# The first stage of a two-layer hybrid backbone: the modulation sums of each quarter are turned between two tiles

## The chip, the core and the metric

The kernel runs on one core of a Trainium2 chip. The core has a matrix engine (TensorE, PE in the profile; its weight loads are PEld), a vector engine (VectorE, DVE), a scalar engine (ScalarE, ACT), GpSimd (POOL) and a sync engine (SyncE, SP) that here only issues loads. Each engine takes its instructions in a fixed order of its own, and they wait for each other by semaphores. The metric is the device time of one execution in microseconds; smaller is better.

## What is computed

Two layers over 512 latent and 256 context tokens of width 1024. The part that matters here is the beginning of layer 0:

```python
sc, scc = silu(c), silu(c_ctx)
m_lat = split(sc @ mod_w[0] + mod_b[0], 6)          # shift, scale, gate, shift, scale, gate
m_ctx = split(scc @ mod_w[0] + mod_b[0], 6)
h_ctx = rms(x_ctx, norm_pre_mix[0]) * (1 + m_ctx[1]) + m_ctx[0]
h_lat = rms(x_lat, norm_pre_mix[0]) * (1 + m_lat[1]) + m_lat[0]
...
gq, gk, gv, gog, gz, aq, ak, av = split(concat(h_ctx, h_lat) @ even_w_in[0], EVEN_SIZES)
```

Behind it come gated linear attention and grouped-query attention side by side, an output projection, a SwiGLU feed-forward, and a second layer with a recurrent mixer (HGRN2) and its feed-forward. All of that stays as it is.

## The kernel before

Tokens lie in six tiles of 128: 0 to 3 are latent, 4 and 5 context. The channels of the 1024 inputs lie in eight blocks `k` of 128, and two blocks make a *quarter* `qd`. To keep float32 accuracy with a faster matmul type, each operand is held as a rounded part H and a remainder L, and a product is three matmuls (`mm3`, line 776): H with H, H with L, L with H. H of a token operand (`x` in the profile) is cast by ACT (`put`, L734) and L subtracted by DVE (L735). H and L of a weight (`wH`, `wL`) are made by ACT (L769) and DVE (L770) from a loaded `raw` buffer.

The first stage (`run`, L1904 to L1989) overlaps three things by quarters:

- `loads(qd)`: SP issues the loads of the modulation weights (`mraw`) and one unit of input weights, for all four quarters at once.
- `sums(qd, ks)`: TensorE sums shift and scale of both streams for this quarter's two channel blocks over the eight input blocks `ks`, 4 matmuls for each (the float32 ones are two passes, so the profile counts 8), into `mod_acc`. Behind the last, `mod_cols` (L465) has DVE copy the sums to `modrows` (L469) and returns a function that makes the *turn*: a transpose on TensorE (`modT`, shown with line 358) and DVE's adding of the bias into `modcol` (L481).
- `apply(qd)`: makes the turn by calling that function (L1942), then DVE forms the factor `aff` (L1945), DVE and ACT scale and shift the quarter's channels of the normalized tokens `xT` (L1954, L1952), and `put` splits the result into H and L.
- `z(t0, qd)`: the products of two token tiles `t0`, `t0`+1 with the quarter's two channel blocks, 2 tiles x 2 blocks x 3 = 12 matmuls of 128 x 288, summed over the quarters in `nat`. The 288 columns are the gates' low-rank input and half of the attention queries.

The last quarter's products are called from `even_mixer` (L1101): behind each pair of tiles ACT copies the results out (`zn` L1103, `natq` L1104). Then come constants for later (`late_constants`, L410): ACT issues the loads of `rows` and of `masks_f`, TensorE transposes the rows (`pt_rows`), DVE copies them to `col` (L408) and casts `masks` (L426); `lower_bounds` (L428) computes with `lb_tmp`. Then the mixer runs pieces in an order that is written out (L1219): `qk0` is two weight units of 1024 columns and the products `gqk`; `m` is one step of sums on DVE (`mod_vec`, L515) for the later modulation vectors: each load `mraw` of 128 x 1024 is multiplied by a column of `scT` and added to two sums `macc` (L535 the first, L537 the others). After eight blocks TensorE adds the sums over the partitions, DVE copies them (`modrows` again, 128 x 512), and TensorE transposes them (`modT` x4).

What sets the order: with `self.pinned` on, TensorE's instructions keep the order of the program (`pin`, L348). The other engines' instructions are placed by the compiler's scheduler, which estimates when each can run; on an engine the order is then fixed. Buffers are few: `raw` has 3, `wH` and `wL` 4 each, the modulation loads of the mixer 3, and a load is issued when its buffer's last reader is done.

## Time and profile before

| what | value |
|---|---|
| three runs | 1681.48, 1681.66, 1682.79 us; median 1681.66 |
| the profiled execution | 1680.08 us, of which the span from the first to the last instruction is 1678.3 us |
| TensorE's mean granted clock | 0.999 |
| transposes and statistics of the input, until the first sums | 0 to 20.6 us |
| the changed stage | 20.6 to 54.8 us |
| the mixer's first products up to the first long turn | 54.8 to 104.8 us |

Rows of the timeline read: start in us, duration in us, engine, line, operation, written tile <- read tiles, partitions x elements and type, count, and in brackets the idle time of the engine ahead of it and what ended it. ACTq and SPq rows are issues of loads. Rows of equal instructions are merged: start of the first, time from there to the end of the last.

### The profile page before, as it was taken

The numbers are of one execution on the slowest core, as the hardware profiler recorded it, in microseconds if no ns is written. First come the engines' busy times: TensorE is split into PE (matmuls) and PEld (weight loads), VectorE is DVE, ScalarE is ACT, GpSimd is POOL, SyncE is SP. The second block draws the span as 40 slices with busy tenths as digits, with TensorE's granted clock in tenths as the row PEclk, the third lists the DMA queues.
The fourth block names the chain that finished last, engine by engine and source line by source line (L and its number), as shares of the span: only waits on it lengthen the run. The fifth ranks groups of instructions, "written<-read, shape, count | busy, mean of one in ns | idle before, by whom it ended". The sixth has DMA issues, their size and how long they took to land.

```text
span 1678.3 us, 32400 instructions
## 1 busy us (share of the span) xinstructions
PE 1638.8 (98%) x13347; PEld 1474.3 (88%) x13347; DVE 1312.2 (78%) x2104; ACT 916.9 (55%) x1560; POOL 122.6 (7%) x129
## 2 busy tenths in 40 slices
PE   6999998999999999999999999999999999999998
PEld 5889987888999999998887788888888899999886
DVE  4889768966898989778668648788775499987887
ACT  4745557846544443445447536566564565555564
POOL 1004210001000000002101000000000100000310
PEclk9999999999999999999999999999999999999999
DMA  9651002154253446249516542111115334433973
GB/s 331 193 155 41 2 28 101 52 198 152 90 151 101 134 148 193 78 136 222 101 56 210 193 132 64 52 54 50 52 56 159 117 113 122 115 101 101 223 166 138
DMA packets 184736, 204.77 MB, mean 122 GB/s; under 512 B 7143, under 2 KB 141837, under 8 KB 184589
## 3 DMA queue, kind: packets, MB, share of 16 engines
q1 hardware_dynamic: 173632, 181.82, 34.6%
q0 software_dynamic: 9024, 17.30, 5.9%
q10 hardware_dynamic: 1932, 3.59, 0.6%
q8 instruction: 104, 1.70, 0.4%
q14 instruction: 44, 0.35, 0.1%
HBM read 193.23 MB, written 9.46 MB: 121 GB/s over the span
## 4 chain that ended last, share of the span: by engine, by line
PE 84%; DVE 7%; ACT 4%; DMA 2%; issue 2%; POOL 1%; DVEq 0%; ACTq 0%; POOLq 0%
PE nat L355 12%; PE a L355 11%; PE ff L355 8%; PE E L355 8%; PE x L355 6%; PE oproj L355 6%; PE o L355 4%; PE b L355 4%; PE D L355 4%; PE pearly L355 3%; PE fq L355 3%; PE gqk L355 2%; PE q L355 2%; PE S L355 2%; PE poh L355 1%
## 5 line engine op out<-in xcount | busy, mean ns | idle before, releaser
L355 PE MATMUL nat<-wH,x 128*128 128x256 f32 (+2 forms) x968 | 226.1, 322 | 3.1 <-ACT x L734 2.6
L355 PEld LDWEIGHTS nat<-wH,x 128*128 128x128 f32 x968 | 162.0, 190 | 20.5 <-ACT x L734 4.2
L824 ACT CAST wH<-raw 128x1024 fp32r<-128x1024 f32 x120 | 124.9, 1051 | 99.0 <-DVE raw L849 37.6
L825 DVE TENSOR_TENSOR wL<-raw,wH 128x1024 fp32r<-128x1024 f32 x120 | 145.7, 1221 | 23.2 <-ACT wH L824 22.6
L355 PE MATMUL nat<-wL,x 128*128 128x256 f32 (+2 forms) x484 | 153.5, 317 | 1.8 <-DVE wL L770 1.8
L770 DVE TENSOR_TENSOR wL<-raw,wH 128x1024 fp32r<-128x1024 f32 (+1 forms) x83 | 98.7, 1198 | 49.7 <-ACT wH L769 49.0
L355 PE MATMUL ff<-x,wH 128*128 128x512 f32 (+1 forms) x512 | 127.7, 340 | 0.0
L769 ACT CAST wH<-raw 128x1024 fp32r<-128x1024 f32 (+1 forms) x83 | 84.9, 1035 | 70.6 <-PE ff L355 19.9
L668 POOL TENSOR_TENSOR rs<-ms,neghalf 128x1 f32<-128x1 f32 (+2 forms) x62 | 64.7, 1049 | 791.1 <-DVE ms L666 791.0
L355 PE MATMUL oproj<-wH,x 128*128 128x512 f32 x320 | 102.3, 396 | 0.6 <-ACT x L1290 0.6
L355 PEld LDWEIGHTS nat<-wL,x 128*128 128x128 f32 x484 | 92.1, 190 | 7.9 <-DVE wL L770 2.7
L355 PEld LDWEIGHTS ff<-x,wH 128*128 128x128 f32 x512 | 87.2, 190 | 10.0
L597 DVE SCALAR_TENSOR_TENSOR macc<-mraw,scT,macc 128x1024 f32<-128x1024 f32 x70 | 88.0, 1280 | 8.8 <-DMA mraw<-in_mod_w_dram 8.4
L355 PE MATMUL x<-wH,two 128*128 128x512 f32 x280 | 90.6, 392 | 0.8 <-DVE y L1801 0.7
L976 ACT COPY qkh<-arr 128x512 f32<-128x512 f32 x112 | 70.1, 642 | 36.4 <-DVE arr L981 32.2
L1723 POOL DMA_DIRECT2D t<-in_ffn_w_down_dram x36 | 41.8, 1198 | 637.2 <-DVE t L1762 337.5
L355 PE MATMUL ff<-x,wL 128*128 128x256 f32 (+1 forms) x256 | 86.2, 337 | 0.0
L849 DVE TENSOR_TENSOR raw<-raw 128x512 f32<-128x512 f32 x120 | 82.8, 690 | 2.8
L981 DVE TENSOR_TENSOR arr<-arr,f 128x512 f32<-128x512 f32 x112 | 74.2, 687 | 1.9 <-ACT qkh L976 0.3
L355 PEld LDWEIGHTS oproj<-wH,x 128*128 128x128 f32 x320 | 59.5, 188 | 12.8 <-ACT x L1290 1.1
L355 PE MATMUL E<-x,wH 128*128 128x384 f32 (+1 forms) x320 | 70.7, 310 | 0.0
L355 PE MATMUL b<-x,wH 128*128 128x384 f32 (+1 forms) x320 | 70.6, 310 | 0.0
(420 smaller groups left out, 4530.2 us busy)
## 6 DMA issues: line engine op xcount, KB each, us to landing
mraw<-in_mod_w_dram SPq DMA_DIRECT2D x80, 512.0 KB, 4.1
raw<-in_ffn_w_gate_dram SPq DMA_DIRECT2D x44, 512.0 KB, 4.8
raw<-in_ffn_w_up_dram SPq DMA_DIRECT2D x44, 512.0 KB, 4.4
raw<-in_odd_w_in_dram SPq DMA_DIRECT2D x40, 512.0 KB, 3.7
t<-in_ffn_w_down_dram POOLq DMA_DIRECT2D x30, 512.0 KB, 8.7
raw<-in_ffn_w_down_dram SPq DMA_DIRECT2D x28, 512.0 KB, 7.9
mraw<-in_mod_w_dram SPq DMA_DIRECT2D x32, 256.0 KB, 6.3
raw<-in_even_w_in_dram SPq DMA_DIRECT2D x16, 512.0 KB, 6.8
```

Source lines behind the costliest of these rows:

```text
L355: return self.pin(self.nc.tensor.matmul(*a, **k))
L597: nc.vector.scalar_tensor_tensor(a, u, w, a, op0=ALU.mult, op1=ALU.add)
L668: nc.gpsimd.tensor_tensor(rs, ms, self.neghalf.to_broadcast([P, w]), op=ALU.pow)
L769: nc.scalar.copy(H[:, :m], raw[:, :m])
L770: nc.vector.tensor_tensor(L[:, :m], raw[:, :m], H[:, :m].bitcast(F32), op=ALU.subtract)
L824: self.nc.scalar.copy(H, f)
L825: self.nc.vector.tensor_tensor(L, f, H.bitcast(F32), op=ALU.subtract)
L849: add = lambda o, x, y: nc.vector.tensor_tensor(o, x, y, op=ALU.add)
L976: nc.scalar.copy(qkv[:, :, :, half, :], dst)
L981: nc.vector.tensor_tensor(dst, dst, tb, op=ALU.mult)
L1723: add = lambda o, src: self.pin(nc.gpsimd.dma_start(out=o, in_=src, accum_op=ALU.add))
```

## The change

Two things. `apply` no longer makes the turn itself, and `z` can do one of its two tiles alone (its results' buffers are then taken by whether they were taken before, not by the quarter). In the loop, the products behind each quarter's second half of sums are cut in two: the first tile, then the turn and `apply`, then the second tile. For the first quarter, the first two of the next quarter's eight blocks are summed ahead of its turn, and the loop's first sums leave these out.

```diff
             def apply(qd):
-                accs[qd]()
                 ks = slice(2 * qd, 2 * qd + 2)
...
-            def z(t0, qd):
+            def z(t0, qd, tiles=(0, 1)):
 
-                if qd == 0:
+                if t0 not in zps:
                     pt = None if t0 == 2 else self.mm_tile("nat")
                     zps[t0] = [self.sc_tile("nat", x) for x in range(2)] if t0 == 2 else [pt[:, :512], pt[:, 512:]]
                 W = zu[qd]
-                for a in range(2):
+                for a in tiles:
                     for k in range(2 * qd, 2 * qd + 2):
...
             sums(0, range(8))
+            sums(1, range(2))
+            accs[0]()
             apply(0)
             for qd in range(1, 4):
-                sums(qd, lo)
+                sums(qd, range(2, 4) if qd == 1 else lo)
                 z(4, qd - 1)
                 if qd < 3:
                     z(0, qd - 1)
                 sums(qd, hi)
-                z(2 if qd < 3 else 0, qd - 1)
+                z(2 if qd < 3 else 0, qd - 1, (0,))
+                accs[qd]()
                 apply(qd)
+                z(2 if qd < 3 else 0, qd - 1, (1,))
             z(2, 2)
```

The instructions are the same in kind and number. Their order changes on three engines at the places below; from the first long turn of the mixer on it is the same as before everywhere.

TensorE, around the turn of the second quarter (`x_354` to `x_355`, after the change `x_363` to `x_364`, are H and L of the tokens; `mraw_275` and `mraw_278` hold the third quarter's modulation weights). Before, from the last block's products of the second tile on:

```order
L355 MATMUL nat<-wH,x_354 128x288
L355 MATMUL nat<-wL,x_354 128x288
L355 MATMUL nat<-wH,x_355 128x288
L358 MATMUL modT<-ident,modrows 128x128
L355 MATMUL mod_acc<-mraw_275,scT 32x128 x8
L355 MATMUL mod_acc<-mraw_278,scT 32x128 x8
```

After, from the last block's products of the first tile on:

```order
L355 MATMUL nat<-wH,x_363 128x288
L355 MATMUL nat<-wL,x_363 128x288
L355 MATMUL nat<-wH,x_364 128x288
L358 MATMUL modT<-ident,modrows 128x128
L355 MATMUL nat<-wH,x_363 128x288
L355 MATMUL nat<-wL,x_363 128x288
L355 MATMUL nat<-wH,x_364 128x288
```

Three more such rows follow there, the second tile's second block, and then the sums of `mraw_275`. The turn (`modT`) has moved ahead of six products.

DVE and ACT, at the first two weight units of `gqk` (rows with `wH` or `wL` of 128x1024; those of 128x576 are the stage's own last unit). ACT before, in the third quarter's `apply`:

```order
L734 CAST x_356<-xT 128x512
L769 CAST wH<-raw 128x576
L734 CAST x_356<-xT 128x512
L769 CAST wH<-raw 128x1024
L405 DMA rows_710<-in_norm_post_mix_dram 16x128
```

ACT after, behind the last products of the stage:

```order
L425 DMA masks_f<-in_const_masks_dram 128x160
L1103 COPY zn<-nat 128x32
L1104 COPY natq<-nat 128x4x64
L1112 DMA wg<-in_gla_w_gate_dram 16x256 x2
L769 CAST wH<-raw 128x1024 x2
L438 ACT_TABLE_LOAD
```

DVE before, from the end of the third quarter's `apply` to the fourth's turn:

```order
L770 TENSOR_TENSOR wL<-raw,wH 128x576
L735 TENSOR_TENSOR x_357<-xT,x_356 128x512
L469 COPY modrows<-mod_acc 128x128
L770 TENSOR_TENSOR wL<-raw,wH 128x1024
L481 TENSOR_TENSOR modcol_236<-modT,col 128x2 x2
```

DVE after, behind the stage's last operand:

```order
L408 COPY col<-pt_rows_718 128x86
L535 TENSOR_SCALAR macc_795<-mraw_792,scT 128x1024
L434 TENSOR_TENSOR lb_tmp<-col 128x16
L535 TENSOR_SCALAR macc_796<-mraw_792,scT 128x1024
L426 CAST masks<-masks_f 128x160
L437 TENSOR_TENSOR lb_tmp<-col,lb_tmp 128x2x8 x2
L537 SCALAR_TENSOR_TENSOR macc_795<-mraw_797,scT,macc_795 128x1024
L770 TENSOR_TENSOR wL<-raw,wH 128x1024 x2
```

The first unit's cast and remainder have moved out of the stage: the cast behind the last copy of its products, the remainder behind the copy of the constants, the cast of the masks and three of the mixer's sums.

DVE at the first long turn (`modrows` of 128x512, for the sums `macc_795` and `macc_796`). Before:

```order
L770 TENSOR_TENSOR wL<-raw,wH 128x1024 x2
L537 SCALAR_TENSOR_TENSOR macc_1291<-mraw_1351,scT,macc_1291 128x1024
L537 SCALAR_TENSOR_TENSOR macc_1292<-mraw_1351,scT,macc_1292 128x1024
L537 SCALAR_TENSOR_TENSOR macc_1291<-mraw_1355,scT,macc_1291 128x1024
L537 SCALAR_TENSOR_TENSOR macc_1292<-mraw_1355,scT,macc_1292 128x1024
L469 COPY modrows<-mod_acc 128x512
```

After:

```order
L770 TENSOR_TENSOR wL<-raw,wH 128x1024
L537 SCALAR_TENSOR_TENSOR macc_1292<-mraw_1355,scT,macc_1292 128x1024
L537 SCALAR_TENSOR_TENSOR macc_1291<-mraw_1359,scT,macc_1291 128x1024
L537 SCALAR_TENSOR_TENSOR macc_1292<-mraw_1359,scT,macc_1292 128x1024
L469 COPY modrows<-mod_acc 128x512
```

Two more sums, those of the load `mraw_1359`, now stand ahead of the copy.

## The prediction

> **What bounds the kernel now.** I read the page first, then the windows of the first 105 us, then the waits of TensorE, then the timeline around each of its waits.

> ```profile
> span 1678.3 us, 32400 instructions
> PE 1638.8 (98%) x13347; PEld 1474.3 (88%) x13347; DVE 1312.2 (78%) x2104; ACT 916.9 (55%) x1560; POOL 122.6 (7%) x129
> 54.80:104.80 50.00, 48.34 (x320) 41.21 (x318) 48.27 (x66) 30.67 (x51) 0.00 (x0) 1.00 0.68 204
> 104.80:1678.30 1573.50, 1549.31 (x12575) 1398.12 (x12575) 1235.52 (x1965) 857.85 (x1452) 117.08 (x113) 1.00 0.39 113
> ```

> TensorE bounds the kernel: it is busy for 98% of the span. The two window rows say more (columns: length, then busy time of PE, weight loads, DVE, ACT, POOL, then granted clock, DMA share, GB/s). From 54.8 to 104.8 us, just behind the stage that is changed, DVE is as full as TensorE, 48.27 against 48.34 of 50 us. What is put off on DVE there isn't made up for free. After 104.8 us DVE has a fifth of its time free.

> In the changed stage TensorE waits for this:

> ```profile
> PE nat L355 <- ACT x L734: 2.6, 4, 0.8
> PE modT L358 <- DVE modrows L469: 0.5, 1, 0.5
> PE nat L355 <- DVE x L735: 0.4, 2, 0.2
> ```

> This view is the waits between 20 and 56 us (total, times, longest). So the most that a better order of the stage can bring is 3.5 us, 0.2% of the run.

> **The change part by part.** All times are those of the profiled execution of the kernel before.

> *First quarter.* The turn waits for a copy, and 16 matmuls (half of the next sums' first half) move ahead of it.

> ```profile
> 23.10 0.30 PE L358 MATMUL modT<-ident,modrows 128*128 128x128 f32 x1 [0.51 <-DVE modrows L469]
> 23.33 1.08 PE L355 MATMUL mod_acc<-mraw,scT 128*32 128x128 f32 x32
> 25.25 0.40 PE L355 MATMUL nat<-wH,x 128*128 128x288 f32 x1 [0.84 <-ACT x L734]
> ```

> 32 of these matmuls take 1.08 us, so the moved ones take 0.54 and fill the wait of 0.51. But the first product comes 2.15 us behind the turn, by a chain on DVE and ACT, and only 0.54 us of work is left ahead of it: the wait of 0.84 grows to about 1.4. The first product stays at 25.25. I take 0; if the 16 matmuls end late the turn is put off by some 0.03, if the copy ended earlier nothing moves. Nothing is gained here.

> *Second and third quarter.* The turn stood behind both tiles' twelve products and now stands behind six.

> ```profile
> 28.84 1.08 PE L355 MATMUL mod_acc<-mraw,scT 128*32 128x128 f32 x32
> 29.99 0.29 DVE L469 COPY modrows<-mod_acc 128x128 f32<-128x128 f32 x1 [1.96 <-PE mod_acc L355]
> 31.55 0.27 PE L358 MATMUL modT<-ident,modrows 128*128 128x128 f32 x1
> 31.76 1.08 PE L355 MATMUL mod_acc<-mraw,scT 128*32 128x128 f32 x32
> 33.62 0.40 PE L355 MATMUL nat<-wH,x 128*128 128x288 f32 x1 [0.78 <-ACT x L734]
> 42.44 0.40 PE L355 MATMUL nat<-wH,x 128*128 128x288 f32 x1 [0.78 <-ACT x L734]
> ```

> The copy that the turn needs is done at 30.28. The twelve products run from 29.85 to 31.55, so six take 0.8 to 0.85, and the turn can stand at 30.75, 0.8 earlier. Turn to first product is 2.07 us (31.55 to 33.62); the cover is now 0.8 of products and 1.08 of sums. The product is ready at 32.82, and TensorE arrives at 32.8: the wait of 0.78 goes. The third quarter has the same pieces and the same 0.78. What is late next is the last product's operand (below); the loads for the sums are not, since the sums start at the same place behind the twelve products as before.

> *Fourth quarter.* Here twelve more products already stand behind the turn.

> ```profile
> 49.19 0.40 PE L355 MATMUL nat<-wH,x 128*128 128x288 f32 x1 [0.21 <-ACT x L734]
> 52.12 0.54 PE L355 MATMUL nat<-wH,x 128*128 128x288 f32 x2 [0.20 <-DVE x L735]
> ```

> With six more the wait of 0.21 goes, and with the chain 0.8 earlier the 0.20 at 52.12 too. Sum of the stage: 0.78 + 0.78 + 0.21 + 0.20 = 1.97 us gained; bounds 1.6 (the arrivals are close to a tie) and 2.4 (each product behind a wait takes 0.40 in place of 0.29). The last products of the stage, ended at 54.75 before, end at 52.8.

> *What the new order does behind the stage.* The first weight unit of the next products (gqk) was cast by ACT and its remainder made by DVE inside the stage:

> ```profile
> 44.22 1.05 ACT L769 CAST wH<-raw 128x1024 fp32r<-128x1024 f32 x1
> 45.78 1.22 DVE L770 TENSOR_TENSOR wL<-raw,wH 128x1024 fp32r<-128x1024 f32 x1
> 54.78 0.71 PE L355 MATMUL gqk<-x,wH 128*128 128x512 f32 x2
> 55.33 0.40 PE L355 MATMUL gqk<-x,wL 128*128 128x512 f32 x1
> ```

> In the changed order the cast stands on ACT behind the last copy out of the stage's products, and the remainder on DVE behind what fills 55.56 to 57.72 below and one more sum. Every third gqk product needs the remainder. The chain there, from its own rows:

> ```profile
> 55.03 0.38 ACT L1104 COPY natq<-nat 128x256 f32<-128x256 f32 x1
> 55.56 0.24 DVE L426 CAST masks<-masks_f 128x160 uint8<-128x160 f32 x1 [3.50 <-DMA masks_f<-in_const_masks_dram]
> 55.72 0.24 DVE L408 COPY col<-pt_rows 128x86 f32<-128x86 f32 x1
> 56.00 0.18 DVE L434 TENSOR_TENSOR lb_tmp<-col 128x16 f32<-128x16 f32 x1
> 56.21 0.26 DVE L437 TENSOR_TENSOR lb_tmp<-col,lb_tmp 128x16 f32<-128x16 f32 x2
> 56.39 1.42 DVE L535 TENSOR_SCALAR macc<-mraw,scT 128x1024 f32<-128x1024 f32 x2
> 57.72 1.22 DVE L770 TENSOR_TENSOR wL<-raw,wH 128x1024 fp32r<-128x1024 f32 x1
> 58.86 1.28 DVE L537 SCALAR_TENSOR_TENSOR macc<-mraw,scT,macc 128x1024 f32<-128x1024 f32 x1
> ```

> The copy of the constants (col) needs a transpose that TensorE does at the end of the stage, at 52.8; from a turn to DVE's next step it is 0.3 (31.55 to the chain's start), so col starts at 53.1. Ahead of the remainder stand, start to start: col 0.28, lb_tmp 0.21 and 0.18, masks 0.16, two sums 1.33, one sum 1.19 (58.86 to the next start at 60.05): 3.35 us. The remainder starts at 56.45 and ends at 57.67. The cast isn't later than that: the last copy moves to 53.1, a cast takes 1.05. So the third gqk product runs at 57.7 in place of 55.33. TensorE, 1.97 ahead, is now **2.4 us behind**; it stands for 4.3 us there, in two pieces with two products between them. Behind it on TensorE stands everything.

> *How much of it is left at 105 us.* There TensorE waited for DVE:

> ```profile
> 99.28 4.87 DVE L537 SCALAR_TENSOR_TENSOR macc<-mraw,scT,macc 128x1024 f32<-128x1024 f32 x4
> 104.07 0.68 DVE L469 COPY modrows<-mod_acc 128x512 f32<-128x512 f32 x1
> 104.81 0.66 PE L358 MATMUL modT<-ident,modrows 128*128 128x128 f32 x4 [1.66 <-DVE modrows L469]
> ```

> TensorE would come at 103.15 + 2.4 = 105.55 and the wait of 1.66 would shrink. DVE: behind the second unit's remainder it went on at 58.86 and reached the copy at 104.07, 45.21 us later, nearly without a pause. In the new order it goes on at 56.45 + 2 x 1.14 = 58.73, has one sum less to do (1.19, done already), and two more sums stand ahead of the copy (2 x 1.20): 58.73 + 45.21 - 1.19 + 2.40 = 105.15. The transpose follows 0.74 later, at 105.89 in place of 104.81: **1.1 us late**, set by DVE, not by TensorE's 105.55. If DVE's one pause of 0.8 goes, TensorE's arrival sets it, 0.7; if the second weight load (its buffer is now free only behind the late remainder) makes DVE wait, up to 1.9.

> *From there to the end* the orders are the same on every engine, and TensorE has the work of 1549 of 1573 us. I carry 1.1 us. Sum: 1678.3 + 1.1 = 1679.4 of span. The profiled execution took 1680.08 with what lies around the span, 1.58 less than the median of the runs, 1681.66; with the same 1.1 the runs come to **1682.8**.

> **The rivals.**

> *The masks land late (slower still).* DVE stood 3.50 us for that load; it was issued at 51.05 and used at 55.56:

> ```profile
> 51.05 0.37 ACTq L425 DMA_DIRECT2D masks_f<-in_const_masks_dram  x1
> 54.16 0.18 ACT L1103 COPY zn<-nat 128x32 f32<-128x32 f32 x1
> ```

> In the new order its issue stands behind the fifth pair of copies, near 54.16 - 1.97 = 52.2. With the same 4.5 us it is there at 56.7, while DVE comes at 53.1 + 0.28 + 0.67 + 0.21 + 0.67 = 54.9. That decides once the load takes over 2.7 us; the price is 1.8 more, 2.9 in all: 1684.6. Against it: before, weights were loaded beside it, and the new order has those loads earlier.

> *The stage gains nothing*, because the loads or ACT set its pace and not the turn: the change doesn't do what it says. Then the same late remainder costs 1.1 + 1.97 = 3.1: 1684.8. Against it: the waits' releasers are all in the chain behind the turn.

> *TensorE's clock falls in the long stand (slower).* The same eight transposes took 1.97 us early on and 1.09 soon after:

> ```profile
> 14.58 1.97 PE L358 MATMUL xT<-ident,xt 128*128 128x128 f32 x8 [0.17 <-DVE ms L666]
> 18.62 1.09 PE L358 MATMUL xT<-ident,xt 128*128 128x128 f32 x8 [0.24 <-DVE xT L1902]
> ```

> So it can run at 1/1.8, from the first matmul at 8.04 to some 17.9. If the stand of 4.3 us brought that back for as long, 9.9 us, 9.9 x (1 - 1.09/1.97) = 4.4 us are lost, TensorE comes at 109.95 and the time is 5.1 up: 1686.8. No wait in the trace after the start is above 1.66, and none changed the clock. [...]

> *The lag is swallowed* by later waits of TensorE that others set (after 105 us the longest are 1.1 to 1.4): 0, 1681.7. Against it: the ones I followed hang on products of TensorE and move with it.

> *The gain is kept* (faster): the late remainder is hidden, and 1.97 stays: 1679.7. For that it would have to be there at 53.4, before the constants' copy that stands ahead of it on DVE.

> **How the numbers follow.** Forecast 0.60, masks 0.12, no gain 0.07, clock 0.06, swallowed 0.11, gain kept 0.04. All but the clock lie within 0.2% (3.4 us), about what a measurement of this kernel can tell from no change. Above it are the clock's larger price and the upper ends of the masks and of no gain with further delays that I haven't found: 0.14 slower. Faster needs more than the whole stage gives: 0.03. Within: 0.83. The range leaves out the kept gain below and the clock above: 1680.6 to 1685.0. The forecast's own range is 1682.3 to 1683.6.

> **What would show it.** Right: in the timeline of the changed kernel the waits of 0.78 at the second and third quarter's first product are gone, the first quarter's is longer than 0.84, the stage's last product ends near 52.8, DVE's first full-width remainder (128x1024) starts near 56.5, and the first gqk product with it stands at about 57.7; the long transpose is near 105.9 with a wait under 0.5, and the span is 1679 to 1680. Wrong: that remainder made before 54 us; the masks' cast released by its load after 56; granted clock under 1.00 behind 53 us; or a wait above 1 us behind 106 us that the kernel before does not have.

## The result, and the profile after

The changed kernel takes 1685.98 us (median of 11 runs, 1684.56 to 1690.04) against 1682.13 us (11 runs, 1680.64 to 1682.79) for the kernel before on the same chip: ratio 1.0028, 95% interval 1.0021 to 1.0036, **3.85 us slower**. The forecast was 1682.8 us, the range 1680.6 to 1685.0.

The profiled execution of the changed kernel took 1686.41 us. First lines of its page:

```profile
span 1684.6 us, 32400 instructions
PE 1641.9 (97%) x13347; PEld 1475.8 (88%) x13347; DVE 1312.9 (78%) x2104; ACT 916.9 (54%) x1560; POOL 122.6 (7%) x129
```

TensorE is busy 3.1 us longer than before (1638.8) with the same 13347 instructions: part of the same work ran slower. DVE and ACT are busy for as long as before.

The timeline of TensorE in the stage, first sums, then the first products of the quarters and the stage's last product:

```profile
20.75 2.39 PE L355 MATMUL mod_acc<-mraw,scT 128*32 128x128 f32 x80
25.36 0.40 PE L355 MATMUL nat<-wH,x 128*128 128x288 f32 x1 [1.28 <-ACT x L734]
32.91 0.40 PE L355 MATMUL nat<-wH,x 128*128 128x288 f32 x1
35.84 0.54 PE L355 MATMUL nat<-wH,x 128*128 128x288 f32 x2 [0.19 <-DVE x L735]
40.95 0.40 PE L355 MATMUL nat<-wH,x 128*128 128x288 f32 x1
52.34 0.29 PE L355 MATMUL nat<-wH,x 128*128 128x288 f32 x1
```

The waits of 0.78 us at the second and third quarter are gone (no bracket at 32.91 and 40.95), the first quarter's has grown from 0.84 to 1.28, and the last product ends at 52.34 + 0.29 = 52.63, 2.3 us earlier than before (54.62 + 0.29 = 54.91 there; the prediction took 54.75, the start of the next transpose). All of this is about as forecast. Then come the constants and the first gqk products, on ACT's queue, TensorE and DVE:

```profile
48.45 0.32 ACTq L405 DMA_DIRECT2D rows<-n_hgrn_lower_bounds_dram  x1
49.83 0.23 ACTq L405 DMA_DIRECT2D rows<-in_hgrn_out_norm_dram  x1
53.35 0.26 PE L358 MATMUL pt_rows<-ident,rows 86*128 86x86 f32 x1 [0.71 <-DMA rows<-n_hgrn_lower_bounds_dram]
53.65 0.25 DVE L408 COPY col<-pt_rows 128x86 f32<-128x86 f32 x1 [3.86 <-PE pt_rows L358]
54.69 0.72 PE L355 MATMUL gqk<-x,wH 128*128 128x512 f32 x2 [1.08 <-ACT wH L769]
56.86 2.35 DVE L770 TENSOR_TENSOR wL<-raw,wH 128x1024 fp32r<-128x1024 f32 x2
58.13 0.80 PE L355 MATMUL gqk<-x,wL 128*128 128x512 f32 x1 [2.72 <-DVE wL L770]
58.73 1.05 PE L355 MATMUL gqk<-x,wH 128*128 128x512 f32 x2
59.58 0.63 PE L355 MATMUL gqk<-x,wL 128*128 128x512 f32 x1
```

The remainder starts at 56.86 (forecast 56.45) and the third product at 58.13 (57.7): also nearly as forecast. But two gqk products behind it take 1.05 us (58.73) where they took 0.71 before (54.78 there), and one takes 0.80 or 0.63 where it took 0.40 (55.33 there). The busy times by stretches say why. The columns are: stretch, its length, busy time and count of PE, PEld, DVE, ACT and POOL, TensorE's granted clock, share of the DMA engines, GB/s.

```profile
48.67:52.09 3.42, 3.35 (x26) 3.12 (x25) 0.69 (x1) 2.33 (x11) 0.00 (x0) 1.00 0.85 295
52.09:55.50 3.41, 1.53 (x8) 0.75 (x6) 1.82 (x6) 2.62 (x5) 0.00 (x0) 1.00 0.14 37
55.50:58.92 3.42, 0.79 (x2) 0.69 (x3) 3.42 (x6) 2.53 (x4) 0.00 (x0) 0.50 0.49 153
58.92:62.33 3.41, 3.41 (x10) 2.64 (x9) 3.41 (x8) 0.00 (x0) 0.00 (x0) 0.50 0.83 241
62.33:65.74 3.41, 3.41 (x19) 2.73 (x18) 2.15 (x4) 1.05 (x1) 0.00 (x0) 1.00 1.00 351
```

From 55.50 to 62.33 us **TensorE ran at half its clock**. The clock record of the trace has this one piece of 6.83 us between the start and the end of the work; before, it has none. The profile is one execution, but the fall is no exception: the mean granted clock was 0.995 to 0.998 in the eleven runs of the changed kernel and 0.997 to 0.999 in the 33 runs of the kernel before that stand beside the first experiments. The averages differ by 0.002, which over 1684 us is what 6.8 us at half clock cost. At the long transpose this is what is left:

```profile
106.91 1.06 PE L355 MATMUL mod_acc<-macc,one 128*32 128x512 f32 x8
108.13 0.69 DVE L469 COPY modrows<-mod_acc 128x512 f32<-128x512 f32 x1
108.88 0.66 PE L358 MATMUL modT<-ident,modrows 128*128 128x128 f32 x4 [0.91 <-DVE modrows L469]
```

It stands at 108.88 in place of 104.81: 4.07 late, against 1.1 in the forecast. Counted from the stage's first sums (20.75; before, 20.64) it is 3.96, and the medians differ by 3.85, so what was lost there was carried to the end. The rest of the profiled execution is no part of the effect: from the long transpose to the last matmul this one took 1567.8 us and the one of before 1565.5, but two further kernels of the experiments with the orders of before behind that point (first quarter alone; early unit, old turns) took 1567.6 and 1566.6.

### The profile page after: what moved, and what is told of

It is laid out like the page before. It is cut to its first block, busy times and chain, and to the rows that moved or that the text cites. A ratio compares the mean times of both kernels' runs of the same rounds, so it can differ in the third digit from the quotient of the medians.

```text
span 1684.6 us, 32400 instructions
## 1 busy us (share of the span) xinstructions
PE 1641.9 (97%) x13347; PEld 1475.8 (88%) x13347; DVE 1312.9 (78%) x2104; ACT 916.9 (54%) x1560; POOL 122.6 (7%) x129
## 4 chain that ended last, share of the span: by engine, by line
PE 81%; DVE 9%; ACT 4%; DMA 3%; issue 2%; POOL 1%; DVEq 0%; ACTq 0%; POOLq 0%
PE nat L355 12%; PE a L355 10%; PE ff L355 8%; PE E L355 7%; PE x L355 7%; PE oproj L355 6%; PE o L355 5%; PE b L355 3%; PE D L355 3%; PE fq L355 3%; PE gqk L355 2%; PE pearly L355 2%; PE q L355 2%; PE S L355 2%; PE poh L355 1%
## 5 line engine op out<-in xcount | busy, mean ns | idle before, releaser
L355 PE MATMUL nat<-wH,x 128*128 128x256 f32 (+2 forms) x968 | 225.8, 321 | 1.6 <-ACT x L734 1.3
L355 PEld LDWEIGHTS nat<-wH,x 128*128 128x128 f32 x968 | 162.1, 190 | 18.5 <-ACT x L734 2.6
L355 PE MATMUL nat<-wL,x 128*128 128x256 f32 (+2 forms) x484 | 153.5, 317 | 1.8 <-DVE wL L770 1.8
L770 DVE TENSOR_TENSOR wL<-raw,wH 128x1024 fp32r<-128x1024 f32 (+1 forms) x83 | 98.9, 1200 | 51.3 <-ACT wH L769 50.5
L355 PE MATMUL ff<-x,wH 128*128 128x512 f32 (+1 forms) x512 | 127.7, 340 | 0.0
L769 ACT CAST wH<-raw 128x1024 fp32r<-128x1024 f32 (+1 forms) x83 | 84.9, 1034 | 76.7 <-PE ff L355 19.7
L355 PE MATMUL oproj<-wH,x 128*128 128x512 f32 x320 | 102.2, 395 | 0.6 <-ACT x L1290 0.6
L355 PEld LDWEIGHTS nat<-wL,x 128*128 128x128 f32 x484 | 92.1, 190 | 7.9 <-DVE wL L770 2.7
L355 PEld LDWEIGHTS ff<-x,wH 128*128 128x128 f32 x512 | 87.3, 190 | 10.0
L355 PE MATMUL x<-wH,two 128*128 128x512 f32 x280 | 90.6, 392 | 0.9 <-DVE y L1801 0.7
L355 PE MATMUL ff<-x,wL 128*128 128x256 f32 (+1 forms) x256 | 86.2, 337 | 0.0
L355 PEld LDWEIGHTS oproj<-wH,x 128*128 128x128 f32 x320 | 59.5, 188 | 12.9 <-ACT x L1290 1.2
L355 PE MATMUL E<-T,wH 128*128 128x384 f32 (+1 forms) x320 | 70.4, 309 | 0.4 <-DVE go L902 0.4
L355 PE MATMUL E<-x,wH 128*128 128x384 f32 (+1 forms) x320 | 70.7, 310 | 0.0
```

The costliest lines, as they stand in the source:

```text
L355: return self.pin(self.nc.tensor.matmul(*a, **k))
L769: nc.scalar.copy(H[:, :m], raw[:, :m])
L770: nc.vector.tensor_tensor(L[:, :m], raw[:, :m], H[:, :m].bitcast(F32), op=ALU.subtract)
```

## The experiments

Theory: the turns gain about 2 us in the stage. The late remainder of the first gqk weight unit takes that back and more, and the fall of the clock in the stand ahead of it adds some 2 us. Against it stand rivals for each part. All diffs are against the changed kernel unless another is named, and each median stands beside that of the kernel before, run in turn with it on the same chip.

### The first quarter's part alone

Against the kernel before, with the other turns made right ahead of each `apply(qd)`, in the same place as there:

```diff
             sums(0, range(8))
+            sums(1, range(2))
+            accs[0]()
             apply(0)
             for qd in range(1, 4):
-                sums(qd, lo)
+                sums(qd, range(2, 4) if qd == 1 else lo)
```

> The kernel before with the first quarter's part alone: its turn of the sums stands behind the first 8 matmuls of the second quarter's sums; the other three turns stay where they were. The orders on DVE, ACT and SP are then those of the kernel before. Theory A (the loss comes from the late remainder of the first gqk weight unit and from TensorE's clock, which fell in the stand ahead of it): neither is there, so no change against the kernel before, within 0.7 us; the granted clock stays 1.00 from 18 us to the end of the matmuls; the wait at the first nat product grows from 0.84 to about 1.3 us. Rival B (the first quarter's part itself costs): 0.5 us or more slower than the kernel before, with the stage's last product later than 54.75.

Measured 1681.75 us against 1681.59 (1.0001, 0.9992 to 1.0010), the mean granted clock of the profiled execution 0.999, as before, the first product's wait 1.28. The first quarter's part is worth nothing; B falls.

### The other three quarters alone

```diff
-            sums(1, range(2))
             accs[0]()
             apply(0)
             for qd in range(1, 4):
-                sums(qd, range(2, 4) if qd == 1 else lo)
+                sums(qd, lo)
```

> The kernel before with the turns of the second, third and fourth quarter moved amid the last two tiles, the first quarter's left where it was. The orders on DVE, ACT and SP are those of the changed kernel. Theory A: all of the loss is here, 3.8 us slower than before (3.0 to 4.6), the first gqk remainder on DVE starts after 56 us, the clock falls to 0.5 between 54 and 58 us for one or two periods of 3.41 us. Rival B (the first quarter's part costs): at least 1 us faster than the changed kernel.

Measured 1686.03 us against 1681.59 (1.0022, 1.0013 to 1.0032): the whole loss. Busy times by stretches, columns as above:

```profile
52.88:56.29 3.41, 1.00 (x3) 0.44 (x3) 2.44 (x8) 2.71 (x5) 0.00 (x0) 1.00 0.14 34
56.29:59.70 3.41, 1.40 (x3) 1.16 (x4) 3.41 (x5) 2.14 (x3) 0.00 (x0) 0.50 0.57 167
59.70:63.12 3.42, 3.42 (x9) 2.64 (x8) 3.42 (x6) 0.00 (x0) 0.00 (x0) 0.50 0.97 309
```

The clock falls at 56.29, again for two stretches of 3.41 us, in the same stand, and the long transpose is as late as in the changed kernel (88.41 us behind the first sums; there 88.13):

```profile
109.31 0.66 PE L358 MATMUL modT<-ident,modrows 128*128 128x128 f32 x4 [0.90 <-DVE modrows L469]
```

### The stand filled with other work

```diff
         self.late_constants()
+        self.spin(8)
+        self.spins = [0, 18]
...
+    def spin(self, n):
+        if n:
+            pt = self.tr_tile("spin")
+            for i in range(n):
+                self.tc.keep_in_program_order(self.nc.tensor.transpose(pt[:, 0:P], self.ident, self.ident))
...
         mm(out, stat[0], mov[1], start=False, stop=False, **k)
+        if self.spins:
+            self.spin(self.spins[1])
+            self.spins = None
```

> The changed kernel with 26 transposes of the identity added on TensorE, whose output nobody reads: 8 behind the transpose of the constants' rows and 18 between the second and the third gqk product, about 1.1 and 2.4 us of work at full clock, in the stand between 52.6 and 58.1 us. The weight unit's remainder on DVE is as late as in the changed kernel. Theory A (the clock's fall is part of the loss): the granted clock stays 1.00, the third gqk product still starts near 58.1 (up to 0.3 later), the products behind it run at 0.68 us for three and not 1.28, the long transpose comes 1.5 to 2.0 us earlier than the 108.88 of the changed kernel, and the time is 1.5 to 2.0 us below the changed kernel's. Rival C (the clock doesn't matter; DVE and the late weight loads set the pace up to the long transpose anyway): the clock stays up too, but the long transpose stays at 108.5 to 109 and the time within 0.5 us of the changed kernel's.

Measured 1684.02 us against 1681.59 (1.0013, 1.0004 to 1.0022), on the same chip **2.0 below** the 1686.03 of the last experiment, which lacks only the first quarter's part. Counted against the kernel before on its own chip each time, the changed kernel lost 3.85 and this one 2.43, which is 1.4 less. Timeline of TensorE, then the busy times by stretches:

```profile
53.45 1.04 PE L783 MATMUL spin<-ident 128*128 128x128 f32 x8
55.47 2.12 PE L783 MATMUL spin<-ident 128*128 128x128 f32 x18
58.14 0.50 PE L355 MATMUL gqk<-x,wL 128*128 128x512 f32 x1 [0.55 <-DVE wL L770]
106.91 0.66 PE L358 MATMUL modT<-ident,modrows 128*128 128x128 f32 x4 [0.90 <-DVE modrows L469]
54.44:57.85 3.41, 2.74 (x21) 2.33 (x20) 3.41 (x8) 3.38 (x5) 0.00 (x0) 1.00 0.39 99
57.85:61.26 3.41, 3.12 (x14) 2.60 (x15) 3.41 (x6) 0.44 (x1) 0.00 (x0) 1.00 0.70 222
```

Work that nobody needs makes the kernel faster. The third product is as late as in the changed kernel (58.14), the clock stays at 1.00, and the long transpose comes 2.0 us earlier than in the changed kernel. C falls: with the clock up, DVE reaches the copy ahead of it earlier too.

### The weight unit early

```diff
...
+        self.late_loads()
+        first = {0: self.unit_cols(w, 0)}
         self.pinned = True
         for t0 in tiles:
             for a, pt in enumerate(z(t0, 3)):
...
-            Ws = {x: self.unit_cols(w, x * P) for x in (c, c + 2)}
+            Ws = {x: first.pop(x) if x in first else self.unit_cols(w, x * P) for x in (c, c + 2)}
```

`late_loads` issues the loads of `rows` and `masks_f`; the transpose, the copy and the cast stay in `late_constants`.

> The changed kernel with the first gqk weight unit, and the loads of the late constants, written ahead of the stage's last products in the program, so that ACT casts the unit ahead of the last six pairs of copies and DVE makes its remainder ahead of the copy of the constants; TensorE's order is that of the changed kernel. Theory A (the turns gain 2 us in the stage, and what turned that into a loss is the late remainder with the clock's fall): the stage's last product ends near 52.6, no stand above 1 us between 52.6 and 60 us, the clock stays 1.00, and the kernel is 0.8 to 2.1 us faster than the kernel before; the exact value hangs on when DVE reaches the copy ahead of the long transpose. Rival D (the stage's gain cannot be kept, since DVE's copy ahead of the long transpose at 104 us comes no earlier): within 0.5 us of the kernel before, with a wait at the long transpose above 3 us. Rival E (the turns gain nothing): the stage's last product ends after 54 us.

Measured **1679.78 us** against 1681.59 (0.9988, 0.9979 to 0.9996): faster than both kernels. Rows of its timeline (its lines L779 and L780 are the old L769 and L770):

```profile
51.60 1.23 DVE L780 TENSOR_TENSOR wL<-raw,wH 128x1024 fp32r<-128x1024 f32 x1 [1.20 <-ACT wH L779]
53.67 0.39 PE L355 MATMUL gqk<-x,wL 128*128 128x512 f32 x1
103.08 0.66 PE L358 MATMUL modT<-ident,modrows 128*128 128x128 f32 x4 [1.66 <-DVE modrows L479]
```

The remainder is made inside the stage, the third product waits for nothing, the clock stays up (mean 0.999, as before). D falls as well: the wait at the long transpose is 1.66, as before, and the transpose itself is earlier. DVE's work up to it begins with the copy of the constants at the end of the stage, and that copy starts at 53.37 us in place of 55.72. E falls: the last product starts at 52.96 and ends at 53.25.

### The same two edits with the old turns, and without the first quarter's part

The first is the last diff made in the kernel before. The second, against the early unit:

```diff
             sums(0, range(8))
-            sums(1, range(2))
             accs[0]()
             apply(0)
             for qd in range(1, 4):
-                sums(qd, range(2, 4) if qd == 1 else lo)
+                sums(qd, lo)
```

> The kernel before, written as the early-unit experiment is: the late constants' loads and the first gqk weight unit ahead of the stage's last products in the program, and the four turns where the kernel before has them. No engine's order differs from that of the kernel before. Theory A (the early-unit kernel is faster because of the turns): the same time as the kernel before, within 0.6 us, and the waits of 0.78 us at the second and third quarter's first product are there. Rival F (the way it is written is what makes it faster): 1 to 2 us faster than before.

> The early-unit experiment without the first quarter's part: that turn is back ahead of all of the second quarter's sums. Theory A (the first quarter's part is worth nothing): 1.3 to 2.3 us faster than before, as the early-unit kernel was (1.8). Rival B' (the first quarter's part holds a share of the gain or takes some of it away): 0.6 us or more from that kernel's gain.

The first took 1682.06 us against 1681.47 (0.9999, 0.9990 to 1.0008), the second 1679.63 against the same 1681.47 (0.9989, 0.9980 to 0.9998). The first one's median is 0.6 above the kernel before, at the edge of what Theory A allowed, and by the ratio there is no difference; F, which needed it to be faster, falls. So the gain of 1.8 us comes from the turns of the quarters two to four, and the way the unit is written only keeps it. In the timeline of the first the old waits are back:

```profile
34.28 0.40 PE L355 MATMUL nat<-wH,x 128*128 128x288 f32 x1 [0.78 <-ACT x L744]
43.11 0.40 PE L355 MATMUL nat<-wH,x 128*128 128x288 f32 x1 [0.78 <-ACT x L744]
```

### What makes the clock fall

Three kernels leave other waits in the stand. The first, against the filled stand:

```diff
-        self.spins = [0, 18]
+        self.spins = [0, 0]
```

The second, against the filled stand:

```diff
-        self.spin(8)
+        self.spin(0)
```

The third, against the changed kernel, cuts the longest wait in pieces with almost no work added. `bounds` is `lower_bounds` made a generator, which hands out columns of `lb_tmp` behind DVE's subtractions and again behind ACT's exponential:

```diff
         mm(out, stat[0], mov[1], start=False, stop=False, **k)
+        if self.touch is not None:
+            self.touches()
...
+    touch = None
+
+    def touches(self):
+        pt = self.tr_tile("touch")
+        self.tr(pt[0:32, 0:P], self.touch, self.ident)
+        self.touch = next(self.bounds)
+        self.tr(pt[0:32, P : 2 * P], self.touch, self.ident)
+        self.touch = None
+        for _ in self.bounds:
+            pass
...
-        self.lower_bounds()
+        self.bounds = self.lower_bounds()
+        self.touch = next(self.bounds)
```

> The changed kernel with 8 transposes of the identity behind the transpose of the constants' rows and none behind the second gqk product, so that one wait of about 2.7 us is left, with more than 1.5 us of nearly unbroken work ahead of it and full work behind it. Theory P (the clock is judged by TensorE's busy share in fixed periods of 3.41 us, and falls below about one half): the wait fills more than half of some period unless a period's end falls near its middle, so the clock falls in about 8 of 10 executions, for one period mostly, and the median is 0.7 to 2.0 us above that of the kernel with the whole stand filled (1684.0). Rival G (it takes 3.4 us without any work): no fall in any execution, 1684.0 within 0.5 us.

> The changed kernel with 18 transposes of the identity behind the second gqk product and none behind the transpose of the rows; waits of about 0.7, 1.1 and 0.5 us are left, with 1.0 us of work between them. Theory P (share of a fixed period): the emptiest period that can lie there is busy for 0.45 to 0.5 of it, so a fall only in a few executions; most at clock 1.00 and the median within 0.6 us of the kernel with the whole stand filled (1684.0). Rival H (any wait of 0.7 us or more with another behind it is enough): the clock falls as in the changed kernel, 1685.5 to 1686.5.

> The changed kernel with two transposes of 32 columns added between the second and the third gqk product, whose output nobody reads: one of lb_tmp as DVE's subtractions leave it, one as ACT's exponential leaves it. They cut the wait of 2.7 us in about 0.5, 1.5 and 0.8 us, so that no wait is longer than the 1.66 us that the kernel before bears without a change of clock, while the busy share hardly grows. Theory P (share of a fixed period): the clock falls as in the changed kernel, and the time is within 0.6 us of its 1686.0. Rival L (the longest single wait decides): no fall, 1.5 to 2.0 us below, near the 1684.0 of the filled stand.

The 3.41 us and the half of Theory P stand in the first two profiles. In the changed kernel's, the clock record has 37.55 us at full clock, then 6.83 at half and 1617.92 at full, which are 11, 2 and 474 times 3.413; in that of the kernel before it has 1655.46 at full, 485 times. Laid on that grid, the period ahead of the fall is busy for 0.45 (1.53 of 3.41), and the emptiest at full clock that no fall follows for 0.54 (1.86 of 3.42, 103.25 to 106.67 us in the kernel before). Rival G takes one such period without any work; the longest wait in these two traces, behind the first sums, is 2.72.

Measured, against 1680.87 us for the kernel before, run in turn with them (0.7 lower than in the experiments up to the early unit): 1685.29 (8 runs; 1.0024, 1.0014 to 1.0034), 1686.09 (6 runs; 1.0030, 1.0018 to 1.0041) and 1684.65 (7 runs; 1.0026, 1.0014 to 1.0037). Busy times by stretches of the first, the one in which the clock was still full and the next:

```profile
53.91:57.33 3.42, 0.91 (x4) 0.30 (x2) 3.42 (x8) 3.37 (x5) 0.00 (x0) 1.00 0.33 89
57.33:60.74 3.41, 3.00 (x7) 2.43 (x8) 3.41 (x6) 0.54 (x1) 0.00 (x0) 0.50 0.73 218
```

of the second:

```profile
52.47:55.89 3.42, 1.64 (x11) 1.33 (x11) 2.61 (x8) 2.87 (x5) 0.00 (x0) 1.00 0.12 34
55.89:59.30 3.41, 3.41 (x16) 3.22 (x15) 3.41 (x5) 2.04 (x3) 0.00 (x0) 0.50 0.62 174
```

and of the third:

```profile
50.92:54.34 3.42, 1.64 (x12) 1.28 (x11) 1.20 (x4) 2.63 (x9) 0.00 (x0) 1.00 0.46 163
54.34:57.75 3.41, 1.93 (x5) 0.81 (x5) 3.41 (x7) 3.30 (x4) 0.00 (x0) 0.50 0.43 131
```

The longest waits in the stand of the first and of the second, and the longest one that is left in the third of the wait of 2.72:

```profile
57.73 0.79 PE L355 MATMUL gqk<-x,wL 128*128 128x512 f32 x1 [2.52 <-DVE wL L770]
54.56 0.73 PE L355 MATMUL gqk<-x,wH 128*128 128x512 f32 x2 [1.35 <-ACT wH L769]
56.79 0.40 PE L358 MATMUL touch<-ident,lb_tmp 128*32 128x128 f32 x1 [1.06 <-ACT lb_tmp L439]
```

G falls: the longest wait in the first kernel is 2.52 us, and the clock fell. L falls as a mechanism: in the second and third no wait in the stand is longer than 1.35, less than the 1.66 that the kernel before bears, and the clock fell all the same. The busy share of the stretch of 3.41 us ahead fits every case, as P says: 0.27, 0.48 and 0.48 in these three, 0.45 in the changed kernel and 0.29 in the quarters two to four, each with a fall behind it, and 0.80 to 0.91 in the filled stand, without one.

The times bear P out only in part. The first is where P put it. The third has the mean granted clocks of the changed kernel (0.995 to 0.998) and is 3.8 us above its kernel before, like the changed kernel's 3.85; but the 1684.65 itself is outside P's 1686.0 within 0.6, and by itself nearer to L's 1684.0. The second missed P's 1684.0 by 2.1 and is where H put it. Its profile shows a fall at a share of 0.48 (1.64 of 3.42), within the 0.45 to 0.5 that I had given for the emptiest period. But this execution, with a mean granted clock of 0.996, is not like the other five: they had 0.998 to 0.999, and the kernel before, run in turn with them, 0.997 to 0.999. So P's fall in a few executions only may well have been right, and the clock doesn't account for the 5.2 us that this kernel lost. Nor is H's mechanism shown by a time alone. In two of the six runs 3.3 and 2.6 us lay outside the span of the instructions, where it is 1.7 to 1.8 in the 15 runs of the kernel before; the spans alone are 4.3 above. Why is open.

## Why the prediction was wrong

The times of the long transpose, counted from the first sums of the same execution, put the parts side by side (each is the difference of two start times in the timelines; the periods are those of 3.41 us at half clock in that stand):

| kernel | first sums to long transpose, us | against before | periods at half clock |
|---|---|---|---|
| before | 84.17 | | 0 |
| early unit | 81.71 | -2.46 | 0 |
| filled stand | 85.96 | +1.79 | 0 |
| second wait filled | 86.80 | +2.63 | 1 |
| first wait filled | 87.40 | +3.23 | 1 |
| wait split | 87.73 | +3.56 | 2 |
| changed kernel | 88.13 | +3.96 | 2 |
| quarters two to four | 88.41 | +4.24 | 2 |

- **First quarter, 0: right.** 1.0001 by itself. In the early unit's profile its part shows 0.5 us (82.24 without it), with a wait of 0.28 for the rows among it; the medians show none (1.81 and 1.84 us gained).
- **Stage, 1.97 gained, bounds 1.6 to 2.4: right, at the upper end.** From the first sums to the last product's end it is 34.27 us before and 31.88 after, 2.4 less. In the end 1.8 of it is to be had (0.7 to 3.5 by the interval of the early unit).
- **The order behind the stage and the late remainder: right.** Forecast 56.45 for its start and 57.7 for the third product, measured 56.86 and 58.13. What was missed is that the loads of the rows don't move with the stage: the last is issued 0.9 earlier than before (49.83, before 50.72), where the stage's end comes 2.3 earlier, and the load that the trace names as the releaser 4.1 later (48.45, before 44.31). So the transpose of the rows waits 0.71 for it.
- **"1.1 us late" at the long transpose: right in kind, too small.** With the clock held up it is 1.8. Counted from the first sums DVE began the remainder there only 0.1 later than I had put it (56.87 less 20.95, against 56.45 less 20.64). But I let it pause no longer than before, one wait of 0.81 for ACT, and in the filled stand it waits for ACT four times, 1.50 us in all.
- **The discounting of the clock: here the step failed.** I gave the fall 0.06 and said that no wait in the trace had changed the clock. The 0.06 rested on how long a single wait must be, and no run shows such a length; what the runs showed is falls behind periods of 3.41 us in which TensorE was busy for 0.27 to 0.48, with longest waits there from 1.22 to 2.74 us. My own forecast had a stand of 4.3 us with one transpose and two products (0.24 + 0.71 us) in it: wherever the periods' borders lie, one period there is at work for about half of its time or less. The price was 2.2 us at the long transpose (88.13 less 85.96) and 1.4 to 2.0 in the medians. Without it the time lies within the stated range: the filled stand's 2.43 above the 1681.66 that the forecast went by is 1684.1.
- **Carried to the end: right.** 3.96 at the long transpose, 3.85 in the medians.

So 1.1 forecast, 0.7 for the undersized lag, 2.2 for the clock: 4.0. The rival that named the clock had a row for the price at hand but worked it out for 9.9 us at low clock; it was 6.83, two periods of 3.41, with TensorE idle for 2.6 of them.

## What to carry to other kernels

A move on one engine that gains time can be lost to what the scheduler then does on the others: compare the orders of all engines, and if a small piece falls behind the stage that gets shorter, write it ahead of that stage's last work (here that turned 3.85 us lost into 1.8 us gained). Several short waits close to each other are to be added up within 3.41 us, the period of the clock records here: TensorE was busy for 0.27 to 0.48 of it ahead of each of the five falls in the stand, and the long transpose came 0.8 to 1.4 us later for each period at half clock than in the filled stand. Count that in before anything else. A quick test of such a loss is to fill the stand with work that nobody reads.

## What the hardware showed that was not expected

```profile
103.25:106.67 3.42, 1.86 (x16) 1.87 (x17) 3.42 (x6) 0.00 (x0) 0.00 (x0) 1.00 0.98 318
102.69:106.10 3.41, 1.69 (x14) 0.76 (x14) 3.41 (x4) 0.59 (x1) 0.00 (x0) 1.00 1.04 358
```

  The clock was 1.00 in the next 3.41 us of both. All through the traces of the kernel before and of the changed kernel it is the same. On the grid that the edges of the clock records give, they have 968 periods at full clock that begin before the last matmul (484 each). The one with 0.45 was followed by half clock, and none of the other 967 was; the two emptiest of these have 0.54, that in the kernel before and one in the changed kernel:

```profile
919.07:922.49 3.42, 1.84 (x7) 1.05 (x6) 3.42 (x4) 3.39 (x6) 0.00 (x0) 1.00 0.80 255
922.49:925.90 3.41, 2.90 (x12) 2.13 (x12) 2.74 (x6) 2.53 (x5) 1.26 (x2) 1.00 0.93 327
```

  The shares are from modelled ends of matmuls, so they are no more exact than that.
- The kernel before comes near the 0.48 itself, with the 0.54 at its wait of 1.66 us ahead of the long transpose. Whether some of its runs lose a period there wasn't tried.
- At half clock, a period with a share of 0.57 (1.93 of 3.41, 54.34 to 57.75 in the split wait) was followed by another at half clock; one with 0.88 (3.00 of 3.41, 57.33 to 60.74 with the first wait filled) was followed by full clock.
